# The second FFN product as one level of Strassen, in both layers of a decoder trunk

## Chip, cores and metric

The kernel runs on one core of a Trainium2 chip. The metric is the device time of one execution in microseconds, given as the median of several runs. All data are float32.

## The reference, cut to what matters

Two layers work on 512 tokens of width 1024. Each has a token mixer (gMLP in layer 0, forgetting attention in layer 1) and then a SwiGLU feed-forward block of hidden width 2816, each between two RMS norms with adaLN shift, scale and gate. After layer 0 the keys, values and forget gates of the attention are projected from the residual stream.

```python
def swiglu(h, w_gu, w_down):
    gu = h @ w_gu
    g, u = jnp.split(gu, 2, axis=-1)
    return (jax.nn.silu(g) * u) @ w_down

h = modulate(rms_norm(x, pre_ffn_g[layer]), sh_f, sc_f)
y = swiglu(h, ffn_w_gu[layer], ffn_w_down[layer])
x = x + g_f[:, None, :] * rms_norm(y, post_ffn_g[layer])
```

The change is to the last product of `swiglu`: 512 x 2816 times 2816 x 1024.

## The kernel before, in words

**Split products.** Every float32 operand of a large product is split into two parts of the type fp32r: `hi` is the rounded copy and `lo` the rest (value minus `hi`). A product takes three matmuls: `hi` by `hi`, `hi` by `lo`, `lo` by `hi`. The copy is mostly on ScalarE (in the profile ACT), the subtraction mostly on VectorE (DVE), in some places on GpSimd (POOL). `load_split` (lines 112 to 123) loads one piece of weights of 128 x 1024 into the tile `raw` by a DMA that SyncE (SP) issues, copies it (L118) and subtracts (L122). `raw` has three buffers in the whole kernel, `whi` and `wlo` two in each pool that has them.

**The FFN** (`ffn`, lines 361 to 413). First product: for each of 22 blocks `m` of 128 hidden columns, a gate and an up product of 24 matmuls of 512 columns each (`prods`, L375), with the normalised input as the moving operand, 16 tiles `hT` of the pool `hp`. `act` (lines 377 to 382) then applies Silu (ACT, L379), multiplies (DVE, L380), and stores the hidden block already split: `hi` by ACT (L381), `lo` by POOL (L382). Between these blocks `run_bg` (L174) issues conditioning work from a queue: `ada_block` (lines 181 to 184) loads 128 x 1024 into `rawb`, which has one buffer, and reduces it on DVE (L184). Inside the FFN's pool the tile is `rawb`; elsewhere it is `raw`. Layer 0 has 64 such blocks in the queue, layer 1 has 8.

**Second product** (lines 406 to 413, `moving`, lines 284 to 322). It is taken in two chunks of 512 output columns. In each, 11 pieces of weights (two k-tiles of 128 rows each) are loaded and split; for every k-tile and each of four token tiles come three matmuls (L300, L301, L302), with the hidden block as stationary operand and the weights moving. That is 2 x 22 x 4 x 3 = 528 matmuls of 512 columns in a layer. Of the second chunk the last six pieces are held on chip (four of them by `load_split_h`, lines 128 to 139, in slots of `hp`) and taken token tile by token tile, so that a tile's sums are complete early.

**After it.** For each token tile `residual` (lines 335 to 352) takes the norm and updates x; in layer 0 `boundary` (lines 415 to 425) then makes the next normalised input of two token tiles at a time (`prenorm_half`, lines 268 to 282: scaling, transposes L277, parts by L252 to L259), under high priority. It also keeps the transposed x in SBUF (L282), for a second normalised input in the attention (lines 798 to 802). The next products (lines 707 to 719) take token tiles 0 and 1 first, then 2 and 3. In layer 1 `residual` stores the output.

**What sets the order.** The program is written in Tile: a scheduler puts each engine's instructions in an order by priority (program order, raised by `high_priority`) and by when it reckons that operands and buffers are ready; on the chip each engine then works through its own list in that order and waits by semaphores. SP's list of DMAs is such a list too.

## Time and profile before

| What | us |
|---|---|
| median of 3 runs | 1394.59 |
| lowest, highest run | 1394.45, 1399.97 |
| profiled execution: span, first to last instruction | 1398.4 |
| busy in it: PE | 1353.1 |
| busy: DVE | 811.5 |
| busy: ACT | 542.1 |
| busy: POOL | 269.1 |

The span is of one profiled execution, and the page gives no other time of it; it lies 3.8 us over the median and inside the range of the runs. PE is TensorE's matmul, PEld its load of the stationary operand. The busy time of an engine is a sum over its instructions; what it waited for is seen in the timeline and in the groups.

### The profile page before, as it was taken

To read this page: it belongs to the slowest core of one execution; us is meant where nothing else is said; L and a number is where in the kernel's file an instruction comes from. 1 tells how busy PE (TensorE), PEld (TensorE's weight loads), DVE (VectorE), ACT (ScalarE), POOL (GpSimd) and SP (SyncE) were. 2 spreads that over 40 slices of the span, in tenths; PEclk is the share of its full clock that TensorE was granted. 3 is DMA by queue.
4 is the path that set the end of the run, shared out by engine and by line. 5 is a ranking of instruction groups with operands and counts; after the bars stand their busy time and mean duration, and the time that the engine had idled before them with its cause. 6 is when DMAs were issued, how large, how long until landed. Compare 5 with 4: busy or idle time off the path is not lost.

```text
span 1398.4 us, 17394 instructions
## 1 busy us (share of the span) xinstructions
PE 1353.1 (97%) x6529; PEld 1126.5 (81%) x6529; DVE 811.5 (58%) x1422; ACT 542.1 (39%) x932; POOL 269.1 (19%) x208
## 2 busy tenths in 40 slices
PE   6999999998999999999999899999989999999998
PEld 4788888778888888778798777888788888888886
DVE  7878857756545556553644857888675232231233
ACT  5234433344223232123653346787543232221231
POOL 4700000013111111000110725563031111110000
PEclk9999999999999999999999999999999999999999
DMA  8565436833666666664123231111326333322231
GB/s 322 169 214 156 135 112 200 276 106 113 211 201 198 196 195 212 222 232 136 53 85 105 76 95 42 31 31 46 109 76 207 116 95 93 103 91 75 91 114 67
DMA packets 55237, 189.08 MB, mean 135 GB/s; under 512 B 6769, under 2 KB 7025, under 8 KB 55154
## 3 DMA queue, kind: packets, MB, share of 16 engines
q1 hardware_dynamic: 54578, 186.93, 42.5%
q8 instruction: 51, 0.84, 0.3%
q10 hardware_dynamic: 576, 1.05, 0.2%
q14 instruction: 32, 0.26, 0.1%
HBM read 185.84 MB, written 2.11 MB: 134 GB/s over the span
## 4 chain that ended last, share of the span: by engine, by line
PE 62%; DVE 6%; DMA 5%; issue 2%; ACT 2%; POOL 0%; DVEq 0%; ACTq 0%; POOLq 0%
PE acc L375 32%; PE acc L301 6%; PE acc L302 5%; PE acc L300 5%; DMA rawb<-in_ada_t 4%; PE acc L860 3%; PE acc L948 1%; PE ps_z L901 1%; DVE wlo L122 1%; PE acc L1080 1%; PE acc L1081 1%; PE acc L1079 1%; PE acc L928 1%; DVE rawb L184 1%; PE ps_x L277 1%
## 5 line engine op out<-in xcount | busy, mean ns | idle before, releaser
L375 PE MATMUL acc<-hT,whi 128*128 128x512 f32 (+1 forms) x1536 | 429.6, 373 | 0.0
L118 ACT ACTIVATE whi<-raw 128x1024 fp32r<-128x1024 f32 (+2 forms) x196 | 204.2, 1043 | 538.5 <-PE acc L375 287.0
L122 DVE TENSOR_TENSOR wlo<-raw,whi 128x1024 fp32r<-128x1024 f32 (+2 forms) x196 | 241.0, 1231 | 242.1 <-ACT whi L118 238.6
L375 PEld LDWEIGHTS acc<-hT,whi 128*128 128x128 f32 x1536 | 273.9, 190 | 49.9
L375 PE MATMUL acc<-hT,wlo 128*128 128x512 f32 (+1 forms) x768 | 268.2, 373 | 0.0
L375 PEld LDWEIGHTS acc<-hT,wlo 128*128 128x128 f32 x768 | 137.8, 191 | 24.9
L382 POOL TENSOR_TENSOR hid<-sg,hid 128x512 fp32r<-128x512 f32 (+1 forms) x48 | 73.9, 1540 | 391.7 <-ACT hid L381 391.7
L301 PE MATMUL acc<-wlo,hT 128*128 128x512 f32 (+1 forms) x352 | 136.0, 386 | 5.0 <-DVE wlo L122 5.0
L302 PE MATMUL acc<-whi,hT 128*128 128x512 f32 (+1 forms) x352 | 135.5, 385 | 0.0
L300 PE MATMUL acc<-whi,hT 128*128 128x512 f32 (+1 forms) x352 | 135.0, 385 | 0.0
L184 DVE CUSTOM_DVE_ANT_0 rawb<-rawb,c_bc 128x1024 f32<-128x1024 f32 x62 | 78.3, 1262 | 95.9 <-DMA rawb<-in_ada_t 63.8
L301 PE MATMUL acc<-wlo,hid 128*128 128x512 f32 x288 | 112.6, 391 | 1.2 <-DVE wlo L122 1.2
L300 PE MATMUL acc<-whi,hid 128*128 128x512 f32 x288 | 112.0, 390 | 1.3 <-ACT junk L327 1.3
L302 PE MATMUL acc<-whi,hid 128*128 128x512 f32 x288 | 112.2, 390 | 0.0
L259 POOL TENSOR_TENSOR hT<-hfull,hT 128x256 fp32r<-128x256 f32 (+1 forms) x43 | 44.0, 1034 | 249.5 <-DVE hT L258 124.8
L301 PEld LDWEIGHTS acc<-wlo,hT 128*128 128x128 f32 x352 | 66.4, 189 | 19.4 <-DVE wlo L122 6.9
L300 PEld LDWEIGHTS acc<-whi,hT 128*128 128x128 f32 x352 | 66.5, 189 | 12.7
L302 PEld LDWEIGHTS acc<-whi,hT 128*128 128x128 f32 x352 | 66.5, 189 | 12.5
L380 DVE TENSOR_TENSOR sg<-sg,acc 128x512 f32<-128x512 f32 (+1 forms) x48 | 30.7, 640 | 78.5 <-PE acc L375 78.5
L122 POOL TENSOR_TENSOR wlo<-raw,whi 128x1024 fp32r<-128x1024 f32 x20 | 55.0, 2752 | 79.0 <-DVE whi L120 47.1
L301 PEld LDWEIGHTS acc<-wlo,hid 128*128 128x128 f32 x288 | 54.1, 188 | 13.9 <-DVE wlo L122 2.8
L300 PEld LDWEIGHTS acc<-whi,hid 128*128 128x128 f32 x288 | 53.9, 188 | 13.2 <-ACT junk L327 1.7
(277 smaller groups left out, 2121.0 us busy)
## 6 DMA issues: line engine op xcount, KB each, us to landing
raw<-in_w_gu SPq DMA_DIRECT2D x88, 512.0 KB, 3.6
raw<-in_ada_t SPq DMA_DIRECT2D x50, 512.0 KB, 4.5
rawb<-in_ada_t SPq DMA_DIRECT2D x46, 512.0 KB, 3.9
raw<-in_w_down SPq DMA_DIRECT2D x44, 512.0 KB, 3.6
raw<-in_w_in SPq DMA_DIRECT2D x32, 512.0 KB, 4.0
raw<-in_w_out SPq DMA_DIRECT2D x16, 512.0 KB, 4.3
rawb<-in_kv_ada_t SPq DMA_DIRECT2D x16, 512.0 KB, 3.7
x<-in_x SPq DMA_DIRECT2D x8, 512.0 KB, 6.1
```

The source lines that it names most:

```text
L118: ACT(hi[:, :width], raw[:, :width], AF.Copy)
L122: lo_eng.tensor_tensor(lo[:, :width], raw[:, :width], f32(hi[:, :width]), sub)
L184: nc.vector.tensor_tensor_reduce(raw, raw, c_bc, 1.0, 0.0, mul, add, dst)
L259: last = lo_eng.tensor_tensor(lo, full, f32(hi), sub)
L277: nc.tensor.transpose(ps[:, i, j * P:(j + 1) * P], xr[j][:, kt * P:(kt + 1) * P], ident)
L300: MM(banks[n], lh, wh, start=kt == 0, stop=False)
L301: MM(banks[n], lh, wl, start=False, stop=False)
L302: MM(banks[n], ll, wh, start=False, stop=kt == kts - 1)
L375: MM(o, (hi, hi, lo)[z][:, ks], h[z == 1][kt][:, cs], start=i == 0, stop=i == 3 * KT - 1)
L380: TT(sg, sg, u, mul)
L382: nc.gpsimd.tensor_tensor(hid[1][m][:, cs], sg, f32(hid[0][m][:, cs]), sub)
L860: pin(MM(box[0], (hi, hi, lo)[z][:, cs], h[z == 1][kt], start=kt + z == 0, stop=kt == KT - 1 and z == 2))
```

## The change

Per layer, the second product is written as one level of Strassen (the form with common sums, after Winograd). The tokens are cut into two halves of 256, the hidden columns into even and odd blocks, the output columns into two halves of 512. Seven products of quarters stand for eight, at the price of sums of quarters of the input (`sums`) and of the weights (`t1` to `t4`), and of sums of the products at the end.

The hidden blocks are no longer stored split. `act` writes float32 quarters (two multiplications of 256 columns), `sums` makes four sums of 128 x 256 on POOL for each pair of blocks, and `down` splits quarters and sums (`parts_q`) as it needs them. `down` has a first loop of 11 pieces with four products each (24 matmuls) in all eight PSUM banks, sums of products, a second loop of 11 pieces with three products each (18 matmuls), of which the last four are held and taken tile by tile, in the order 2, 3, 0, 1. The kept transposed x goes to DRAM and back. The next products take token tiles 2 and 3 first. In layer 0 the queue of conditioning work is emptied faster: 67 of its 68 entries in the first product instead of 57. `down` runs inside the pool that has `rawb`. The diff, cut to this (it also takes away comments and docstrings, and passes `y0` tile by tile elsewhere):

```diff
-                nc.scalar.copy(keep[kp][:, :, cs], ps)
+                kst = small.tile([P, 2, 256], F32, name="kst", tag="t2", bufs=3)
+                nc.scalar.copy(kst, ps)
+                nc.sync.dma_start(keep[kp][:, :, cs], kst)
...
-    def residual(n, y0, ps, ss, row, sx):
+    def residual(n, y0, ps, ss, row, sx, raw=1):
...
-            TT(y1, ps, row[:, 512:1024], mul)
+            TT(y1, ps, row[:, raw * 512:raw * 512 + 512], mul)
...
-        for j, y in enumerate((y0[:, n, :], y1)):
+        for j, y in enumerate((y0, y1) if raw else (y1, y0)):
...
+    def down(src, qa, qb, fp, fw, row, done):
+        H = 256
+        NP = NF // 2
+        TAIL = 4
+        ss = fw.tile([P, 2 * NT], F32, name="ss", bufs=1)
+        X, Z = ([acc.tile([P, 512], F32, name="acc") for _ in range(2)] for _ in range(2))
+        Y, W = ([aux.tile([P, 512], F32, name="ps_x", tag=t) for _ in range(2)] for t in ("ps_t", "ps_s"))
+        def parts(w, lo_eng=nc.vector, held=False):
+            if not held:
+                hi, lo = (hp.tile([P, S], F32R, name="hT") for _ in range(2))
+            else:
+                q = held_tile("wq", F32R)
+                hi, lo = q[:, 0], q[:, 1]
+            ACT(hi, w, AF.Copy)
+            lo_eng.tensor_tensor(lo, w, f32(hi), sub)
+            return hi, lo
+        def parts_q(q, n, held):
+            if held:
+                hi, lo = (fp.tile([P, 1024], F32R, name="qh", tag="qb", bufs=NP)[:, :n * H] for _ in range(2))
+            else:
+                hi, lo = (wp.tile([P, 1024], F32R, name=t, tag=t, bufs=2)[:, :n * H] for t in ("whi", "wlo"))
+            ACT(hi, q, AF.Copy)
+            TT(lo, q, f32(hi), sub)
+            return lambda i, t: tuple(x[:, i * H + t * P:i * H + t * P + P] for x in (hi, lo))
+        def prod(bank, a, w, start, stop):
+            (ah, al), (wh, wl) = a, w
+            MM(bank, ah, wh, start=start, stop=False, skip_group_check=True)
+            MM(bank, ah, wl, start=False, stop=False, skip_group_check=True)
+            MM(bank, al, wh, start=False, stop=stop, skip_group_check=True)
+        def half_piece(i):
+            r0 = raw_tile()
+            nc.sync.dma_start(r0[:, :512], src[0, i, :, 512:])
+            return r0[:, :512]
+        def held_tile(name, dt=F32):
+            return fp.tile([P, 2, 512], dt, name=name, tag="qa", bufs=NP)
+        for i in range(NP):
+            r0, r1 = raw_tile(), raw_tile()
+            nc.sync.dma_start(r0, src[0, i])
+            nc.sync.dma_start(r1, src[1, i])
+            t1, t2 = (t[:, z] for t in (fw.tile([P, 2, 512], F32, name="ta", tag="whi"),) for z in range(2))
+            t4 = fw.tile([P, 2, 512], F32, name="tb", tag="wlo")[:, 0]
+            TT(t1, r1[:, :512], r0[:, :512], sub)
+            nc.gpsimd.tensor_tensor(t2, r1[:, 512:], t1, sub)
+            nc.gpsimd.tensor_tensor(t4, r0[:, 512:], t2, sub)
+            a = parts_q(qa[i].rearrange("p q c -> p (q c)"), 4, False)
+            for z, (w, bank, eng) in enumerate(((r0[:, :512], X, nc.vector), (t1, Z, nc.vector), (t2, Y, nc.vector),
+                                                (t4, W, nc.gpsimd))):
+                w = parts(w, eng)
+                for t in range(2):
+                    prod(bank[t], a((3, 1, 2, 0)[z], t), w, i == 0, i == NP - 1)
+            run_bg(1)
+        u2 = held_tile("u2")
+        uw = [held_tile("uw") for _ in range(2)]
+        for t in range(2):
+            nc.scalar.copy(u2[:, t], X[t])
+        for t in range(2):
+            TT(u2[:, t], Y[t], u2[:, t], add)
+        for t in range(2):
+            TT(uw[t][:, 1], Z[t], u2[:, t], add)
+            TT(uw[t][:, 0], W[t], u2[:, t], add)
+        V = [aux.tile([P, 512], F32, name="ps_x", tag="ps_t") for _ in range(2)]
+        held = []
+        for i in range(NP):
+            last = i >= NP - TAIL
+            r1 = raw_tile()
+            nc.sync.dma_start(r1, src[1, i])
+            t3 = fw.tile([P, 2, 512], F32, name="ta", tag="whi")[:, 0]
+            nc.gpsimd.tensor_tensor(t3, r1[:, 512:], r1[:, :512], sub)
+            a = parts_q(qb[i].rearrange("p q c -> p (q c)")[:, H:], 3, last)
+            b22 = parts(r1[:, 512:], held=last)
+            if last:
+                held.append([i, a, b22, parts(t3)])
+                continue
+            b21, w3 = parts(half_piece(i), nc.gpsimd), parts(t3)
+            for t in range(2):
+                prod(Z[t], a(1, t), b22, False, False)
+            for t in range(2):
+                prod(X[t], a(2, t), b21, False, False)
+            for t in range(2):
+                prod(V[t], a(0, t), w3, i == 0, False)
+            run_bg(1)
+        for h in held:
+            h.append(parts(half_piece(h[0]), nc.gpsimd, held=True))
+        g = row()
+        for t in range(2):
+            for i, a, b22, w3, b21 in held:
+                prod(V[t], a(0, t), w3, False, i == NP - 1)
+            n = 2 + t
+            TT(uw[t], V[t].unsqueeze(1).broadcast_to([P, 2, 512]), uw[t], add)
+            sumsq(uw[t][:, 1], ss[:, 2 * n:2 * n + 1])
+            TT(uw[t][:, 1], uw[t][:, 1], g[:, 512:], mul)
+            done(n, uw[t][:, 0], uw[t][:, 1], ss, g, 0)
+        for t in range(2):
+            for i, a, b22, w3, b21 in held:
+                prod(Z[t], a(1, t), b22, False, i == NP - 1)
+            TT(u2[:, t], Z[t], u2[:, t], add)
+            sumsq(u2[:, t], ss[:, 2 * t:2 * t + 1])
+            TT(u2[:, t], u2[:, t], g[:, 512:], mul)
+            for i, a, b22, w3, b21 in held:
+                prod(X[t], a(2, t), b21, False, i == NP - 1)
+            done(t, X[t], u2[:, t], ss, g, 0)
+    def ffn(layer, h, row, done, halves=(0, 1)):
-            hid = [[fp.tile([P, S], F32R, name=f"hid{q}_{m}") for m in range(NF)] for q in range(2)]
+            qa, qb = ([fp.tile([P, 4, H], F32, name=f"q{z}{i}", tag=f"q{z}", bufs=NF // 2) for i in range(NF // 2)]
+                      for z in "ab")
...
-                    TT(sg, sg, u, mul)
-                    ACT(hid[0][m][:, cs], sg, AF.Copy)
-                    nc.gpsimd.tensor_tensor(hid[1][m][:, cs], sg, f32(hid[0][m][:, cs]), sub)
+                    i = m // 2
+                    outs = ((qb[i][:, 3], qa[i][:, 0]) if m % 2 else (qa[i][:, 3], qb[i][:, 0]))
+                    for z, half in enumerate(range(cs.start // H, cs.stop // H)):
+                        TT(outs[half], sg[:, z * H:z * H + H], u[:, z * H:z * H + H], mul)
+                def sums(i):
+                    a22, s1, s2, a11 = (qa[i][:, z] for z in range(4))
+                    a21, s3, s4, a12 = (qb[i][:, z] for z in range(4))
+                    for o, x0, x1, op in ((s1, a21, a22, add), (s2, s1, a11, sub), (s3, a11, a21, sub), (s4, a12, s2, sub)):
+                        nc.gpsimd.tensor_tensor(o, x0, x1, op)
...
+                sums(0)
...
                             with behind_norm():
-                                run_bg(1 if layer else 1 + j)
+                                run_bg(1 if layer else 1 + j + (m % 2) * (1 - j))
                         ps.append(b)
                     act(m, ps[0], ps[1], slice(0, S))
+                    if m % 2:
+                        sums(m // 2)
+                down(w_down[layer], qa, qb, fp, fw, row, done)
                 bgp.pop()
-            with tc.tile_pool(name=f"fd{layer}", bufs=1) as fd:
-                y0 = fd.tile([P, NT, 512], F32, name="y0")
-                ss = fd.tile([P, 2 * NT], F32, name="ss")
-                lhs = hl(hid)
-                moving([w_down[layer, 0, i] for i in range(NF // 2)], NF, 512, lhs, first_half(y0, ss, row))
-                moving([w_down[layer, 1, i] for i in range(NF // 2)], NF, 512, lhs,
-                       lambda n, ps: done(n, ps, y0, ss, row()), tail=6,
-                       tail_load=lambda i, src: load_split_h(src) if i > 1 else cols_of(load_split(src), 512))
...
-        def done(n, ps, y0, ss, row):
+        def done(n, ps, y0, ss, row, raw=1):
...
-                residual(n, y0, ps, ss, row, sx)
+                residual(n, y0, ps, ss, row, sx, raw)
                 xrs(n, sx, rst)
-                if n == 1:
-                    box.append(new_h())
                 if n % 2:
-                    prenorm_half(n // 2, rst, box[0], a, b, keep() if keep else None)
+                    if not box:
+                        box.append(new_h())
+                    prenorm_half(n // 2, rst, box[0], a, b, keep)
...
+    keep = [dram.tile([P, 2, S], F32, name=f"keep{i}", bufs=1) for i in range(4)]
...
-            for grp in ((0, 1), (2, 3)):
+            for grp in ((2, 3), (0, 1)):
...
+                kept = raw_tile().rearrange("p (a s) -> p a s", a=2)
+                nc.sync.dma_start(kept, keep[kt // 2])
                 full2 = small.tile([P, 2, S], F32, name="full2", tag="t4", bufs=2)
-            evac_h(h, kt, slice(0, S), keep[kt // 2][:, kt % 2, :], A1, B1, nc.scalar, nc.vector, nc.gpsimd,
+            evac_h(h, kt, slice(0, S), kept[:, kt % 2, :], A1, B1, nc.scalar, nc.vector, nc.gpsimd,
                    full2[:, kt % 2, :])
```

## Rows read from the trace of the kernel before

**Rows 1.** The core's span (us) and its granted TensorE clock.
```profile
core 0: 1398.4 us, clock 0.988
```

**Rows 2.** The page, part 4: the chain that ended last, by engine.
```profile
PE 62%; DVE 6%; DMA 5%; issue 2%; ACT 2%; POOL 0%; DVEq 0%; ACTq 0%; POOLq 0%
```

**Rows 3.** Windows, second product, each layer: us; PE, PEld, DVE, ACT, POOL busy; clock, DMA, GB/s.
```profile
565.70:691.80 126.10, 123.31 (x545) 100.08 (x544) 64.23 (x115) 39.11 (x66) 3.93 (x4) 1.00 0.50 161
1271.70:1391.60 119.90, 119.90 (x529) 98.78 (x527) 36.03 (x53) 28.48 (x43) 1.29 (x1) 1.00 0.27 88
```

**Rows 4.** Groups of instructions by shape, 1271.7 to 1391.6 us: busy us, mean ns | idle.
```profile
L301 PE MATMUL acc<-wlo,hid 128*128 128x512 f32 x144 | 56.1, 390 | 0.0
L122 DVE TENSOR_TENSOR wlo<-raw,whi 128x1024 fp32r<-128x1024 f32 x16 | 19.6, 1225 | 64.0 <-ACT whi L118 64.0
L118 ACT ACTIVATE whi<-raw 128x1024 fp32r<-128x1024 f32 x16 | 17.0, 1061 | 63.7 <-PE acc L302 63.7
L137 DVE TENSOR_TENSOR hT<-raw,hT 128x512 fp32r<-128x512 f32 x8 | 5.1, 684 | 1.6 <-ACT hT L135 1.6
L135 ACT ACTIVATE hT<-raw 128x512 fp32r<-128x512 f32 x8 | 4.6, 620 | 2.4 <-DMA raw<-in_w_down 2.4
L382 POOL TENSOR_TENSOR hid<-sg,hid 128x512 fp32r<-128x512 f32 x1 | 1.3, 1287 | 9.1 <-ACT hid L381 9.1
```

**Rows 5.** Lines L785 (VectorE) and L788 (GpSimd), side by side: ns min/median/max, first and last start.
```profile
L785 DVE TENSOR_TENSOR k<-k,r x8: 683/1782/1796, 770.9 to 800.4; 128x512 f32<-128x512 f32 x8
L785 DVE TENSOR_TENSOR q<-q,r x4: 682/683/693, 821.9 to 823.8; 128x512 f32<-128x512 f32 x4
...
L788 POOL TENSOR_TENSOR k<-k,kq x8: 1620/1742/2262, 772.7 to 803.3; 128x512 f32<-128x512 f32 x8
```

**Rows 6.** Timeline of the start, 43 to 50 us, VectorE and GpSimd: start, length.
```profile
44.35 2.22 DVE L459 SCALAR_TENSOR_TENSOR A_m<-A_m,b,colv 128x1 f32<-128x1 f32 x1
46.50 1.21 DVE L454 CUSTOM_DVE_ANT_0 raw<-raw,c_bc 128x1024 f32<-128x1024 f32 x1
47.76 1.13 DVE L460 TENSOR_TENSOR B_m<-B_m,colv 128x1 f32<-128x1 f32 x1
...
43.25 3.31 POOL L122 TENSOR_TENSOR wlo<-raw,whi 128x1024 fp32r<-128x1024 f32 x1 [1.51 <-DVE whi L120]
46.52 2.35 POOL L259 TENSOR_TENSOR hT<-hfull,hT 128x512 fp32r<-128x512 f32 x1
49.57 3.30 POOL L122 TENSOR_TENSOR wlo<-raw,whi 128x1024 fp32r<-128x1024 f32 x1 [0.70 <-DVE whi L120]
```

**Rows 7.** Tile rawb, layer 0: ns min/median/max, first and last start; time to landing.
```profile
L184 DVE CUSTOM_DVE_ANT_0 rawb<-rawb,c_bc x54: 1212/1226/1920, 337.4 to 624.9; 128x1024 f32<-128x1024 f32 x54
DMA to landing us min/median/max: 3.3/3.9/5.0
```

**Rows 8.** The page, part 6: loads of the second product, KB each, us to landing.
```profile
raw<-in_w_down SPq DMA_DIRECT2D x44, 512.0 KB, 3.6
```

**Rows 9.** Timeline after token tile 1's last product in layer 0, by engine.
```profile
674.32 0.57 ACT L327 ACTIVATE junk<-acc 128x512 bf16<-128x512 f32 x1
...
687.84 1.32 POOL L259 TENSOR_TENSOR hT<-hfull,hT 128x256 fp32r<-128x256 f32 x1 [117.88 <-DVE rq L169]
695.11 0.81 POOL L259 TENSOR_TENSOR hT<-hfull,hT 128x256 fp32r<-128x256 f32 x1 [0.32 <-DVE rq L168]
...
696.38 0.88 DVE L122 TENSOR_TENSOR wlo<-raw,whi 128x704 fp32r<-128x704 f32 x1
```

**Rows 10.** Timeline of the end: the last product and the last update of x.
```profile
1391.42 0.39 PE L302 MATMUL acc<-hT,hid 128*128 128x512 f32 x1
1394.08 1.42 DVE L348 SCALAR_TENSOR_TENSOR x<-y,rpost,x 128x512 f32<-128x512 f32 x2
```

**Rows 11.** Window 30 to 40 us, columns as in rows 3.
```profile
30.00:40.00 10.00, 6.59 (x21) 4.69 (x21) 9.89 (x11) 2.15 (x4) 9.30 (x4) 0.83 0.72 256
```

More of the change, by code (lines that the diff above doesn't have):

```diff
@@ L126, in cols_of @@
         return lambda j: tuple(t[:, j * nw:(j + 1) * nw] for t in hl_)
-    def load_split_h(src):
-        raw = raw_tile()
-        nc.sync.dma_start(raw, src)
-        parts = []
-        for j in range(2):
-            hi = hp.tile([P, S], F32R, name="hT")
-            ACT(hi, raw[:, j * 512:(j + 1) * 512], AF.Copy)
-            lo = hp.tile([P, S], F32R, name="hT")
-            TT(lo, raw[:, j * 512:(j + 1) * 512], f32(hi), sub)
-            parts.append((hi, lo))
-        return lambda j: parts[j]
     def rsqrt(dst, s0, s1, width):
@@ L358, in hl @@
         return lambda kt, n: (h[0][kt][:, n * P:(n + 1) * P], h[1][kt][:, n * P:(n + 1) * P])
-    def ffn(layer, h, row, done):
+    def down(src, qa, qb, fp, fw, row, done):
[99 more added lines that the diff above has]
+            done(t, X[t], u2[:, t], ss, g, 0)
@@ L363, in ffn @@
+    def ffn(layer, h, row, done, halves=(0, 1)):
+        H = 256
         with tc.tile_pool(name=f"ffn{layer}", bufs=1) as fp:
-            hid = [[fp.tile([P, S], F32R, name=f"hid{q}_{m}") for m in range(NF)] for q in range(2)]
+            qa, qb = ([fp.tile([P, 4, H], F32, name=f"q{z}{i}", tag=f"q{z}", bufs=NF // 2) for i in range(NF // 2)]
+                      for z in "ab")
             with tc.tile_pool(name=f"fw{layer}", bufs=2) as fw:
@@ L379, in act @@
                     ACT(sg, g, AF.Silu)
-                    TT(sg, sg, u, mul)
-                    ACT(hid[0][m][:, cs], sg, AF.Copy)
-                    nc.gpsimd.tensor_tensor(hid[1][m][:, cs], sg, f32(hid[0][m][:, cs]), sub)
+                    i = m // 2
[7 more added lines that the diff above has]
+                        nc.gpsimd.tensor_tensor(o, x0, x1, op)
                 ws = [[load_split(w_gu[layer, m, j], pool=(wp, fw)[m], hi_eng=(None, nc.vector)[m],
                                   lo_eng=(nc.vector, nc.gpsimd)[m]) for j in range(2)] for m in range(2)]
-                for half in range(2):
+                for half in halves:
                     cs = slice(half * 256, half * 256 + 256)
@@ L655, in tile_yoco_trunk @@
         moving([w_out[1, i] for i in range(8)], NG, 512, lambda kt, n: (vh[:, kt, n, :], vl[:, kt, n, :]),
-               lambda n, ps: d0(n, ps, y0, ss, g_m0[0]), tail=5,
+               lambda n, ps: d0(n, ps, y0[:, n, :], ss, g_m0[0]), tail=5,
                tail_load=lambda i, src: cols_of(load_split(src, pool=gp, bufs=5), 512),
@@ L668, in tile_yoco_trunk @@
     kbox = []
-    kp = {}
-    def keep():
-        if not kp:
-            kp["ctx"] = tc.tile_pool(name="attk", bufs=1, side="right")
-            ap = kp["ctx"].__enter__()
-            kp["t"] = [ap.tile([P, 2, S], F32, name=f"keep{i}") for i in range(4)]
-        return kp["t"]
+    keep = [dram.tile([P, 2, S], F32, name=f"keep{i}", bufs=1) for i in range(4)]
     ffn(0, hbox[0], lambda: (run_bg(100), g_f0[0])[1], boundary(sx2, rst2, kbox, Ak, Bk, keep))
-    keep = kp["t"]
     with tc.tile_pool(name="att", bufs=1) as tp:
@@ L799, in tile_yoco_trunk @@
             if kt % 2 == 0:
+                kept = raw_tile().rearrange("p (a s) -> p a s", a=2)
+                nc.sync.dma_start(kept, keep[kt // 2])
                 full2 = small.tile([P, 2, S], F32, name="full2", tag="t4", bufs=2)
-            evac_h(h, kt, slice(0, S), keep[kt // 2][:, kt % 2, :], A1, B1, nc.scalar, nc.vector, nc.gpsimd,
+            evac_h(h, kt, slice(0, S), kept[:, kt % 2, :], A1, B1, nc.scalar, nc.vector, nc.gpsimd,
                    full2[:, kt % 2, :])
-        kp["ctx"].__exit__(None, None, None)
         outer = tp
@@ L1084, in tile_yoco_trunk, with store @@
                         else:
-                            d2(n, bank, y0, ss, g_m1[0])
+                            d2(n, bank, y0[:, n, :], ss, g_m1[0])
     g_f1 = gate_row("f1", ("a", 1, 5), C_POSTF + 8)
-    def store(n, ps, y0, ss, row):
-        residual(n, y0, ps, ss, row, None)
+    def store(n, ps, y0, ss, row, raw):
+        residual(n, y0, ps, ss, row, None, raw)
     ffn(1, fbox[0], lambda: (run_bg(100), g_f1[0])[1], store)
```

## Prediction

> **What bounds the kernel now.** I read the span first: 1398.4 us at a granted clock of 0.988, so full speed (2.4 GHz) nearly throughout [rows 1]. The profiled run lies 3.8 us over the median of 1394.59; I work out a difference against the span and put it on the median. The chain that ended last is PE for 62% [rows 2], so the next view is the two windows of the second FFN product. In layer 1 PE is busy for all of 119.90 us; in layer 0 for 123.31 of 126.10, with DVE busy for half of the time [rows 3]. Of the 529 matmuls in layer 1's window 528 are the product: 119.90 / 529 = 0.2267 us each. The groups of that window show its split work with room to spare: a DVE subtraction of 1024 columns takes 1.225 us, of 512 columns 0.684; the ACT copies take 1.061 and 0.620; a POOL subtraction of 512 columns, alone, 1.287 [rows 4]. PE sets this stage today, and the reader has to ask whether it still will once there is less for PE and more for the others.
>
> **What goes.** Per layer 7 x 11 x 2 x 3 = 462 matmuls stand for 528. The 66 saved are 66 x 0.2267 = 15.0 us, in both layers 29.9: the whole gain.
>
> **What comes, first loop** (11 pieces of 24 matmuls, 24 x 0.2267 = 5.44 us of PE each). Per piece DVE has one subtraction of 1024 columns (the quarters) and four of 512 (t1 and three lo parts): 1.225 + 4 x 0.684 = 3.96 us. POOL has three of 512 (t2, t4, one lo): 3 x 1.287 = 3.86. ACT has 1.061 + 4 x 0.620 = 3.54. Each engine by itself is below 5.44. But each of these DVE and POOL instructions reads two operands in SBUF, and the trace shows that such instructions don't run side by side. Lines L785 (DVE) and L788 (POOL) work next to each other: the DVE one then takes 1.78 us, against 0.683 when POOL is quiet, and the POOL one 1.742, against 1.287 alone [rows 4, 5]. In the start of the kernel a DVE instruction on one element per partition takes 2.22 us: it begins at 44.35 in the middle of a POOL subtraction and ends with it, at 46.57 against 46.56; then L454, begun first, holds up POOL's next one, which takes 2.35 [rows 6]. So their times add. A pair of 512 columns takes 1.742 where the two alone make 0.684 + 1.287 = 1.971: a share of 0.884, since the ends overlap a little. I take this share for all, as rows 5 show the same two kinds of instruction: (3.96 + 3.86) x 0.884 = 6.9 us for a piece, over PE's 5.44. The bounds are 5.44 (no adding up) and 7.82 (the full sum).
>
> The Trainium skill (SBUF — State Buffer, Who interferes with whom) says that a VectorE instruction with two SBUF inputs and a GpSimd instruction that reads SBUF exclude each other for the whole instruction. By that a piece would take the full 7.82 us where the row gives 6.9; what that makes of the time is a rival below, and the pair in rows 5 speaks for 6.9.
>
> The head start is one piece: its `hT` slots and temporaries come free in the last 5.4 us of the first product, so 1.5 of its 6.9 us are left when PE arrives. The last weight sum of piece 10 is ready at 1.5 + 10 x 6.9 = 70.5 us, PE then has 6 matmuls left and ends the loop at 71.9, against 59.8 for PE alone.
>
> **Sums of products.** Two ACT copies and six DVE additions, of which PE has to wait for some 2 us (two to three additions of 0.684 before it may go on in Z). This hides: the second loop's first piece isn't ready before 70.5 + 4.3 = 74.8. If PE set the pace it would cost the 2 us.
>
> **Second loop** (18 matmuls, 4.08 us of PE a piece). DVE: 768 columns, which no row has; between 0.88 for 704 and 1.225 for 1024 [rows 4, 9] I take 0.95, nearest to the first; and two of 512. POOL: two of 512. Together 0.95 + 1.37 + 2.57 = 4.89, times 0.884 = 4.33, again over PE. Piece 6 is ready at 70.5 + 7 x 4.33 = 100.8. The four held pieces need 0.95 + 1.37 + 1.29 = 3.61, times 0.884 = 3.19 each before V can be finished: 113.6. The first thing that PE's list has after piece 6 is V of the held pieces, so it waits for them. Then 3 matmuls and 60 more: 63 x 0.2267 = 14.3, end at 127.9. Before it was 119.9: **8 us longer** in each layer.
>
> **The end of a tile.** A tile of the lower half now needs an addition of 1024 columns and a gain more on DVE, about 1.9 us, and four tiles come 2.7 us apart or 5.4, not 8.2. The queue on DVE makes the last update of x about 1 us later than today's 1394.08 - 1391.42 = 2.7 us after the last product [rows 10]. Layer 1: 8 + 1 = +9.
>
> **Conditioning blocks in layer 0.** They go through one buffer: 54 begin from 337.4 to 624.9, one in 5.42 us, with 3.9 us of that for the load [rows 7]. Issuing them earlier in the program doesn't speed up a ring of one buffer, and ten or so that used `raw` now use it too. 64 at 5.42 us end at 678.9; the second product begins at 565.7 [rows 3], so 21 of them fall into it. Before, DVE had 62 us of idle time there. Now each holds the shared path for 1.226 x 0.884 = 1.08 us: +23 us. Bounds: 0 (all hidden in waits) and 21 x 2 = 42 (DVE also stands before each one until its load lands, with the splits queued behind it).
>
> **The boundary after layer 0.** From tile 1's last product to the last part of the next input of that half 21.6 us pass (674.32 to 695.92) [rows 9]. Covering it were the 72 matmuls of tiles 2 and 3 (16.3 us); now it is the 48 of tiles 0 and 1 (10.9). The next product can begin on its first k-tiles, so I take 4 of the missing 5.4 us. Bounds 0 and 10, as DVE now has more queued there.
>
> **Priced at nothing.** The hidden block's second multiplication and POOL's four sums of 256 columns (0.81 each [rows 9]) take the place of a copy and a split, under 48 matmuls (10.9 us) a block. The kept x: the ACT copy stays, eight stores of 256 KB and four loads of 512 KB (3.6 us to land [rows 8]) stand in SP's list by weight loads that are due 16 us later; without that cover a load's 3.6 us. Loads of weights: 1 MB in 6.9 us is 152 GB/s, below the 161 that layer 0 has today [rows 3]. PSUM: the next product waits until X is read; within the boundary's bounds.
>
> **Sum:** 9 + 8 + 23 + 4 = +44 us: 1394.6 + 44 = **1439 us**.
>
> **Rivals.**
> - *PE stays the limit* (faster). DVE and POOL overlap enough that a piece of the first loop needs under 5.44 us, 70% of the full sum; that is the point from which it decides. For it: each engine alone has 30% idle, and PE alone is the chain today. Against it: rows 5 and 6. Then -29.9, two waits of 2 for sums of products, two ends of 1 and 4 at the boundary: -20, 1375 us. Chance 0.18.
> - *In between.* Handing over is cheaper and a piece takes 6.0 us, and the blocks of layer 0 hide: 9 + 8 + 4 - 2 x 9 = +3, 1398 us. Chance 0.07.
> - *The blocks hide, the rest stands.* +21, 1416 us. Rows 7's 3.9 us of load leave DVE free to split meanwhile. Chance 0.12.
> - *The ring of three `raw` buffers.* Each piece takes two, and the next r1 goes into the buffer that t4 of this one frees: t1, t2, t4 and a load are 0.68 + 1.29 + 1.29 + 3.6 = 6.9 us [rows 4, 8] with nothing in between; with two other DVE instructions let in first, 0.6 each, 8.1. Then 10 x 1.2 us more a layer: +68, 1463 us. Chance 0.12.
> - *Full exclusion*, 7.82 and 4.89 us a piece, and 3.61 a held one: the first loop's last sum at 2.4 + 78.2 = 80.6, the held pieces at 80.6 + 34.2 + 14.4 = 129.2, end at 143.5, that is +23.6 a layer for +8, and 3 for the blocks: +78, 1473 us. Chance 0.08. This is the rule named above (Trainium skill, SBUF — State Buffer) taken to the letter.
>
> PE's pauses could also bring its clock down: in one window with PE busy for 6.59 of 10 us the grant is 0.83, so part of it at 1.2 GHz [rows 11]. In the first loop PE would be busy for 5.44 of 6.9 us. I put up to 10 us for it into the upper end only.
>
> **How the numbers follow.** The forecast, 1416 to 1456 by its own bounds, has 0.43. The range goes from 1392 (in between, less a few us) to 1476 (ring and most of full exclusion) and leaves out the fast rival and a little above. This kernel can tell 0.5%, 7 us, from no change: faster 0.18, same 0.07, slower 0.12 + 0.43 + 0.12 + 0.08 = 0.75.
>
> **What would show it.** In the changed profile: PE busy near 80% in the first loop with waits for DVE or POOL subtractions; POOL's 512-column subtractions at about 1.7 us and many DVE ones over 1 us; one idle stretch of PE some 10 us long, all told, ahead of the held pieces; `rawb` still loading in layer 0's second product. I am wrong if PE is dense in both loops (then POOL at 1.29 and DVE at 0.68), or if its waits end on a load of `raw` (the ring).

## The result, and the profile after

The changed kernel takes 1458.9 us (median of 4 runs, 1458.41 to 1459.71) against 1395.66 for the kernel before beside it: a ratio of 1.0439, 95% interval 1.0415 to 1.0462. It is slower by 63 us where the prediction said 44; 1458.9 lies in its wide range of 1392 to 1476, and just above the 1416 to 1456 that the forecast gave itself by its own bounds. The profiled run is the 1458.41 one, its span 1456.7 us, 58.3 over the span of [rows 1].

The chain that ended last in the kernel after, by engine (before: [rows 2]):

```profile
PE 35%; DVE 11%; issue 5%; POOL 4%; ACT 3%; DMA 3%; DVEq 0%; POOLq 0%; ACTq 0%; SPq 0%
```

PE's share falls from 62% to 35%. To find where the 58.3 us lie, cut the span at the same events in both kernels: first and last matmul of each second product, and the last of the first v products. Windows of the kernel after, columns as in [rows 3]: layer 0's second product, from its end to the end of the first v products, layer 1's second product, its first loop alone, what follows that loop, and the end.

```profile
563.30:718.80 155.50, 122.06 (x463) 92.27 (x462) 144.59 (x152) 64.95 (x102) 90.08 (x56) 0.91 0.61 197
718.80:772.90 54.10, 40.26 (x226) 38.36 (x227) 33.63 (x96) 31.70 (x70) 11.45 (x12) 0.84 0.35 113
1315.00:1446.80 131.80, 112.84 (x463) 85.60 (x461) 115.44 (x114) 66.36 (x110) 91.17 (x56) 0.99 0.46 142
1315.00:1390.70 75.70, 64.84 (x266) 49.39 (x264) 67.74 (x56) 36.71 (x57) 59.82 (x37) 0.98 0.48 146
1390.70:1446.80 56.10, 47.99 (x199) 36.21 (x197) 47.70 (x59) 29.65 (x54) 31.36 (x20) 1.00 0.43 136
1446.80:1456.70 9.90, 0.00 (x0) 0.00 (x0) 6.75 (x17) 1.61 (x5) 0.00 (x0) 0.66 0.43 159
```

The kernel before has the second of these as:

```profile
691.80:728.20 36.40, 34.53 (x211) 34.15 (x211) 20.42 (x57) 21.75 (x43) 7.62 (x10) 0.95 0.32 99
```

| stretch | before | after | difference | predicted |
|---|---|---|---|---|
| up to layer 0's second product | 565.7 | 563.3 | -2.4 | 0 |
| layer 0, second product | 126.1 | 155.5 | +29.4 | +31 |
| boundary and first v products | 36.4 | 54.1 | **+17.7** | +4 |
| attention, layer 1's first product | 543.5 | 542.1 | -1.4 | 0 |
| layer 1, second product | 119.9 | 131.8 | +11.9 | +8 |
| end | 6.8 | 9.9 | +3.1 | +1 |
| span | 1398.4 | 1456.7 | +58.3 | +44 |

(58.3 and not 63, mostly as the profiled run of before was 3.8 us over the median.) In layer 1's product the count of matmuls fell by 66, yet the product takes 11.9 us more: PE is busy for only 112.84 of 131.80 us, DVE for 115.44 (36.03 of 119.90 before [rows 3]). What each does in the first loop, groups by shape (the last column is idle time and what ended it):

```profile
L371 DVE TENSOR_TENSOR hT<-ta,hT 128x512 fp32r<-128x512 f32 x21 | 30.6, 1457 | 5.9 <-ACT hT L370 5.4
L371 POOL TENSOR_TENSOR hT<-tb,hT 128x512 fp32r<-128x512 f32 x11 | 20.9, 1904 | 7.5 <-ACT hT L370 7.5
L388 PE MATMUL acc<-hT,wlo 128*128 128x512 f32 x44 | 18.7, 425 | 9.0 <-DVE wlo L381 9.0
L405 POOL TENSOR_TENSOR ta<-raw,ta 128x512 f32<-128x512 f32 x10 | 16.0, 1603 | 6.8 <-DVE ta L404 6.8
L406 POOL TENSOR_TENSOR tb<-raw,ta 128x512 f32<-128x512 f32 x10 | 16.0, 1599 | 0.7
L404 DVE TENSOR_TENSOR ta<-raw 128x512 f32<-128x512 f32 x10 | 13.2, 1324 | 1.2 <-DMA raw<-in_w_down 0.8
L371 DVE TENSOR_TENSOR hT<-raw,hT 128x512 fp32r<-128x512 f32 x12 | 12.2, 1017 | 0.9 <-PE ps_x L387 0.7
```

A subtraction of 512 columns that takes DVE 0.684 us alone [rows 4] takes 1.02 to 1.46 in the mean here, POOL's 1.60 to 1.90 for 1.287. Only 0.8 us of DVE's idle time ahead of t1 ends on a load; PE's longest wait ends on DVE's part of the quarters (L381). The timeline shows them taking turns:

```profile
1338.33 1.68 POOL L405 TENSOR_TENSOR ta<-raw,ta 128x512 f32<-128x512 f32 x1 [0.62 <-DVE ta L404]
1339.03 1.52 DVE L371 TENSOR_TENSOR hT<-ta,hT 128x512 fp32r<-128x512 f32 x1 [0.18 <-ACT hT L370]
1340.09 1.63 POOL L406 TENSOR_TENSOR tb<-raw,ta 128x512 f32<-128x512 f32 x1
1340.71 1.55 DVE L371 TENSOR_TENSOR hT<-ta,hT 128x512 fp32r<-128x512 f32 x1 [0.15 <-ACT hT L370]
```

POOL's first ends at 1340.01, DVE's at 1340.55; POOL's second at 1341.72, DVE's at 1342.26. Each DVE instruction ends 0.54 us after the POOL one beside which it began, as if it did its work once POOL is through. From the first matmul of piece 1 (1321.1) to that of piece 10 (1382.8) are nine pieces of 6.85 us, predicted 6.9. In the second loop POOL stands 11.6 us, all told, ahead of the sum t3 for loads of `raw`; no run sets apart what that costs.

In layer 0's second product the blocks go on loading, 21 of them as predicted, the last at 716.5 us (tile rawb):

```profile
L171 DVE CUSTOM_DVE_ANT_0 rawb<-rawb,c_bc x21: 1198/1214/2348, 567.0 to 716.5; 128x1024 f32<-128x1024 f32 x21
```

That blocks run into this product is not new: in the kernel before 18 began in it, the last at 624.9 [rows 7], and PE was still busy for 123.31 of 126.10 us [rows 3]. What is new is that DVE is full there.

And the boundary, the stretch that was mis-sized. DVE after the V products of tiles 2 and 3, with the first part of the next input, and PE's first v product:

```profile
708.11 1.23 DVE L451 TENSOR_TENSOR uw<-ps_x,uw 128x1024 f32<-128x1024 f32 x1 [0.82 <-PE ps_x L388]
709.25 1.21 DVE L171 CUSTOM_DVE_ANT_0 rawb<-rawb,c_bc 128x1024 f32<-128x1024 f32 x1
711.00 1.77 DVE L453 TENSOR_TENSOR uw<-uw,grow 128x512 f32<-128x512 f32 x1
712.69 1.24 DVE L151 SCALAR_TENSOR_TENSOR rq<-ss 128x1 f32<-128x1 f32 x1
716.45 1.20 DVE L171 CUSTOM_DVE_ANT_0 rawb<-rawb,c_bc 128x1024 f32<-128x1024 f32 x1
719.38 0.75 DVE L338 SCALAR_TENSOR_TENSOR x<-y,rpost,x 128x512 f32<-128x512 f32 x1
724.45 0.75 DVE L338 SCALAR_TENSOR_TENSOR x<-y,rpost,x 128x512 f32<-128x512 f32 x1
733.07 0.27 DVE L245 CAST hT<-hfull 128x256 fp32r<-128x256 f32 x1
733.40 0.66 PE L817 MATMUL acc<-whi,hT 128*128 128x352 f32 x1
```

The sum of tile 2 begins at 708.11, its x at 719.38, tile 3's at 724.45. PE ends the product at 718.8 and begins the next at 733.40; in between it has only transposes. Two blocks, and two instructions held up while POOL has the path (1.77 us, and 1.24 for one element per partition), stand in DVE's queue. In the first v products, 733.4 to 772.9, PE waits for the split v weights (us in total, times, longest):

```profile
PE acc L817 <- ACT whi L118: 1.7, 1, 1.7
PE acc L818 <- DVE wlo L122: 1.3, 2, 0.7
```

### The profile page after: what moved, and what is told of

Its sections match the earlier page's. It is cut to its first block, busy times and chain, and to the rows that moved or that the text cites. A ratio compares the mean times of both kernels' runs of the same rounds, so it can differ in the third digit from the quotient of the medians.

```text
span 1456.7 us, 17922 instructions
## 1 busy us (share of the span) xinstructions
PE 1349.4 (93%) x6397; PEld 1108.9 (76%) x6397; DVE 999.8 (69%) x1606; ACT 599.5 (41%) x1034; POOL 488.4 (34%) x358
## 4 chain that ended last, share of the span: by engine, by line
PE 35%; DVE 11%; issue 5%; POOL 4%; ACT 3%; DMA 3%; DVEq 0%; POOLq 0%; ACTq 0%; SPq 0%
PE acc L482 15%; PE acc L963 3%; DVE hT L371 2%; DMA raw<-in_w_down 2%; PE acc L290 1%; PE acc L291 1%; PE acc L289 1%; PE acc L1051 1%; PE ps_z L1004 1%; POOL tb L406 1%; POOL ta L405 1%; DVE wlo L122 1%; DVE wlo L381 1%; PE acc L1183 1%; ACT hT L370 1%
## 5 line engine op out<-in xcount | busy, mean ns | idle before, releaser
L118 ACT ACTIVATE whi<-raw 128x1024 fp32r<-128x1024 f32 (+2 forms) x160 | 166.0, 1039 | 438.0 <-PE acc L482 303.5
L122 DVE TENSOR_TENSOR wlo<-raw,whi 128x1024 fp32r<-128x1024 f32 (+2 forms) x160 | 196.6, 1230 | 145.1 <-ACT whi L118 143.1
L171 DVE CUSTOM_DVE_ANT_0 rawb<-rawb,c_bc 128x1024 f32<-128x1024 f32 x72 | 101.1, 1404 | 73.5 <-DMA rawb<-in_ada_t 49.7
L371 DVE TENSOR_TENSOR hT<-ta,hT 128x512 fp32r<-128x512 f32 x66 | 89.8, 1364 | 9.1 <-ACT hT L370 8.2
L496 POOL TENSOR_TENSOR qa<-qb,qa 128x256 f32<-128x256 f32 x22 | 35.7, 1625 | 172.5 <-DVE qa L490 172.5
L496 POOL TENSOR_TENSOR qb<-qa,qb 128x256 f32<-128x256 f32 x22 | 35.7, 1622 | 159.1 <-DVE qb L490 159.1
L388 PE MATMUL acc<-hT,wlo 128*128 128x512 f32 x144 | 61.8, 431 | 27.5 <-DVE wlo L381 27.5
L290 PEld LDWEIGHTS acc<-wlo,hT 128*128 128x128 f32 x352 | 66.4, 189 | 17.8 <-DVE wlo L122 5.2
L370 ACT ACTIVATE hT<-ta 128x512 fp32r<-128x512 f32 x66 | 41.5, 629 | 87.7 <-DVE ta L404 52.5
L386 PE MATMUL acc<-hT,whi 128*128 128x512 f32 x144 | 60.2, 418 | 12.0 <-DVE uw L421 6.7
L387 PE MATMUL acc<-hT,whi 128*128 128x512 f32 x144 | 59.8, 415 | 3.8 <-POOL hT L371 2.6
```

The costliest lines, as they stand in the source:

```text
L118: ACT(hi[:, :width], raw[:, :width], AF.Copy)
L122: lo_eng.tensor_tensor(lo[:, :width], raw[:, :width], f32(hi[:, :width]), sub)
L171: nc.vector.tensor_tensor_reduce(raw, raw, c_bc, 1.0, 0.0, mul, add, dst)
L290: MM(banks[n], lh, wl, start=False, stop=False)
L371: lo_eng.tensor_tensor(lo, w, f32(hi), sub)
L386: MM(bank, ah, wh, start=start, stop=False, skip_group_check=True)
```

## The experiments

**1. All subtractions of the second product on DVE.**

```
-nc.gpsimd.tensor_tensor(t2, r1[:, 512:], t1, sub)
-nc.gpsimd.tensor_tensor(t4, r0[:, 512:], t2, sub)
+TT(t2, r1[:, 512:], t1, sub)
+TT(t4, r0[:, 512:], t2, sub)
```

(and so for t3 and the lo parts of t4 and b21)

> All the subtractions of the second product that POOL had (t2, t4, t3 and the lo parts of t4 and b21) go to DVE; POOL has none left there. Theory (DVE and POOL take turns on a shared path, so that their times add): a piece of the first loop then costs DVE 3.96 + 3 x 0.684 = 6.0 us with nothing beside it, against 6.9 now, although DVE has more to do; its 512-column subtractions fall from 1.0 to 1.5 us to 0.68. In layer 1 the first loop goes from 75.7 us to 66 to 69, the second product from 131.8 to 117 to 121; in layer 0 the second product from 155.5 to 139 to 144; the kernel from 1459 to 1426 to 1435. Rival 1 (the engines work independently, and DVE's long times are its own): DVE gets three more of 1.36 us a piece, 6.6 + 4.1 = 10.7, the first loop of layer 1 takes over 110 us and the kernel over 1520. Rival 2 (the buffers of the loads set the pace): DVE goes on waiting and the kernel stays within 10 us of 1459.

Measured: 1417.1 us, ratio to before 1.0145 (1.0122 to 1.0168), 42 us below the changed kernel. Windows of layer 1's second product and of its first loop, then a whole piece on DVE:

```profile
1294.30:1405.20 110.90, 107.36 (x463) 87.39 (x461) 106.25 (x167) 65.81 (x110) 3.25 (x3) 0.98 0.52 171
1294.30:1354.20 59.90, 59.90 (x266) 49.51 (x265) 58.53 (x86) 35.31 (x56) 3.25 (x3) 1.00 0.55 180
```

```profile
1320.13 1.22 DVE L381 TENSOR_TENSOR wlo<-qa,whi 128x1024 fp32r<-128x1024 f32 x1
1321.27 0.69 DVE L371 TENSOR_TENSOR hT<-ta,hT 128x512 fp32r<-128x512 f32 x1
1321.87 0.68 DVE L371 TENSOR_TENSOR hT<-tb,hT 128x512 fp32r<-128x512 f32 x1
...
1325.62 1.22 DVE L381 TENSOR_TENSOR wlo<-qa,whi 128x1024 fp32r<-128x1024 f32 x1
```

With more to do, DVE is faster: eight instructions in 5.49 us, and PE is dense in the first loop (59.9 of 59.9 us, 5.45 a piece). Layer 1's product takes 110.9 us, less than the 117 to 121 expected, and the kernel less than its 1426 to 1435; layer 0's product, 138.2, comes out just under its 139 to 144. The reason: a DVE instruction of 0.68 us begins 0.60 us after the one ahead of it, that of 1.22 is followed after 1.14. So the 6.0 us that was added up from durations is really 1.14 + 7 x 0.60 = 5.3, below PE's 5.44. Rivals 1 and 2 fall.

**2. Subtractions on POOL that nobody needs,** on top of experiment 1.

```
+for _ in range(3):
+    nc.gpsimd.tensor_tensor(tb[:, 1], r1[:, 512:], r0[:, 512:], sub)
```

> All subtractions of the second product on DVE, and POOL gets three subtractions of 512 columns for each piece of the first loop whose result nobody reads, as many as it had there. Theory (taking turns on a shared path): they still cost, though nothing waits for them: a piece of the first loop goes from 5.45 us to 8.2 to 9.0, DVE's 512-column subtractions from 0.685 to 1 us or more in the mean; the kernel from 1417 to 1475 to 1500. Rival (what cost 6.9 us was the chain t1, t2, t4 that went from DVE to POOL and back, its latency and its waits): the piece stays at 5.4 to 5.6 us and the kernel at 1417 to 1423.

Measured: 1482.8 us (one run); a piece of layer 1's first loop takes 8.9 us (1334.8 to 1414.8 for nine). Groups in that loop:

```profile
L409 POOL TENSOR_TENSOR tb<-raw 128x512 f32<-128x512 f32 x30 | 49.7, 1657 | 35.5 <-DMA raw<-in_w_down 30.4 <-DVE hT L371 3.6
L371 DVE TENSOR_TENSOR hT<-ta,hT 128x512 fp32r<-128x512 f32 x23 | 25.8, 1129 | 0.0
L406 DVE TENSOR_TENSOR ta<-raw,ta 128x512 f32<-128x512 f32 x10 | 16.9, 1694 | 0.0
```

No result of L409 is read, and each of the three costs a piece (8.9 - 5.45) / 3 = 1.15 us. So it is the shared path, not the chain over two engines. Nor is it the loads that POOL's reads of `raw` might hold back: DVE is busy for 78.5 of these 80.0 us.

**3. The sums left out.**

```
-nc.gpsimd.tensor_tensor(t2, r1[:, 512:], t1, sub)
-nc.gpsimd.tensor_tensor(t4, r0[:, 512:], t2, sub)
+t2, t4 = r1[:, 512:], r0[:, 512:]
...
-nc.gpsimd.tensor_tensor(t3, r1[:, 512:], r1[:, :512], sub)
+t3 = r1[:, :512]
```

> Leaves out the sums t2, t4 and t3 (raw quarters are multiplied in their place), and the lo parts that POOL had go to DVE: the same number of matmuls and of loads, but DVE has 3.96 + 0.684 = 4.6 us a piece in the first loop and 3.0 in the second, POOL nothing. Theory (the shared path of DVE and POOL sets the pace, not PE, the loads or the buffers): PE sets the pace, 5.44 and 4.08 us a piece; layer 1's second product takes 105 to 109 us for 131.8 now, layer 0's 116 to 123 for 155.5, the kernel 1390 to 1402. Rival (the loads' buffers or PE's clock set the pace): pieces of the first loop stay above 6.3 us and the kernel above 1430.

Measured: 1430.9 us (one run), layer 1's product 122.0 us, a piece 6.11: a miss, and in the kernel's time (above 1430) what the rival said, though the piece stays below its 6.3. With less work than in experiment 1 it is slower. Groups of layer 1's first loop:

```profile
L380 ACT ACTIVATE whi<-qa 128x1024 fp32r<-128x1024 f32 x9 | 9.5, 1052 | 10.2 <-PE ps_x L387 10.2
L404 DVE TENSOR_TENSOR ta<-raw 128x512 f32<-128x512 f32 x10 | 6.9, 692 | 15.0 <-DMA raw<-in_w_down 15.0
```

DVE stands 15.0 us ahead of t1 until a load lands (0.8 in the changed kernel). The edit changed more than it meant to: t2 and t4, as tiles of their own, had set `raw` free early; now the raw quarters stay until their parts are made, and these wait for slots that PE frees. That is read from the trace alone; a run with a fourth raw buffer, which would test it, was not made. Since the edit opened a new wait, the run decides neither for the theory nor against it.

**4. The last 22 conditioning blocks left out.**

```
+nblk[0] += 1
+if 42 < nblk[0] <= 64:
+    nc.vector.memset(dst, 0.0)
+    return
```

> Leaves out the last 22 conditioning blocks of layer 0 (their loads and their reductions; zeros stand in their columns), which are those that fall into its second product. Theory (each holds the shared path, which sets the pace there): layer 0's second product falls from 155.5 us to layer 1's 130 to 134, and the stretch from its end to the end of the first v products from 54.1 to 46 to 50, as three of the blocks stand in front of the updates of x there; the kernel takes 1427 to 1433. Rival (DVE does them in waits that it has anyway): the product stays at 150 or more, the kernel at 1452 or more.

Measured: 1434.4 us (one run), 24.0 below the profiled run of the changed kernel. Windows of the product and of the boundary:

```profile
564.40:704.10 139.70, 116.77 (x467) 87.89 (x465) 117.19 (x121) 71.58 (x121) 89.81 (x56) 0.96 0.45 143
704.10:748.60 44.50, 38.23 (x221) 36.26 (x222) 26.75 (x77) 24.76 (x52) 11.54 (x12) 0.92 0.40 129
```

The size of the term was right (+23), though the kernel came out just above its 1427 to 1433. By these windows 15.8 us come out of the product (130 to 134 was expected, it is 139.7) and 9.6 out of the boundary (44.5, for 46 to 50). But the cut misleads here: ahead of the last five matmuls of the product PE stands 4.5 us for the scaled x of the next input, a wait of the boundary that now lies in the product. From the product's first matmul to the sum of tile 2 it took 144.8 us and now takes 119.5; from that sum to the first v product it took 25.3 and takes 25.7 (4.5 of them DVE stands for a part of the v weights). So all of the gain lies ahead of that sum.

**5. The edits of experiments 1 and 4 together.**

```
-nc.gpsimd.tensor_tensor(t2, r1[:, 512:], t1, sub)
+TT(t2, r1[:, 512:], t1, sub)
...
+if 42 < nblk[0] <= 64:
+    nc.vector.memset(dst, 0.0)
+    return
```

> Both edits: all subtractions of the second product on DVE, and the last 22 conditioning blocks of layer 0 left out (zeros in their columns). Theory: both layers' second products take 117 to 121 us; the stretch from the end of layer 0's to the end of the first v products falls from 54.1 to 42 to 47, because neither blocks nor POOL stand in DVE's way, and what is left over the 36.2 us of before is the shorter cover (48 matmuls for 72, 5.4 us); the kernel takes 1395 to 1404. Rival for that stretch (the order of the tiles and the cover alone make the delay, not DVE's backlog): it stays at 51 us or more, here and without the blocks alone.

Measured: 1386.6 us (one run), below the kernel before. The products take 108.1 and 111.1 us, below what was expected for the reason found in experiment 1. But the boundary keeps 50.3: there the theory missed, and the rival (51 or more) came close in this run, though not in experiment 4 (44.5), to which it also laid claim. DVE's backlog is the smaller part of the boundary's loss: 3.8 of 17.7 us go with it.

**6. The blocks early.** All subtractions on DVE, nothing left out.

```
-raw = bgp[-1].tile([P, 1024], F32, name="rawb", bufs=1) if bgp else raw_tile()
+if bgp and len(bg) % 3:
+    raw = small.tile([P, D], F32, name="rawt", tag="t4", bufs=2)
+else:
+    raw = bgp[-1].tile([P, 1024], F32, name="rawb", bufs=1) if bgp else raw_tile()
-run_bg(1 if layer else 1 + j + (m % 2) * (1 - j))
+run_bg(1 if layer else 2)
```

> All subtractions of the second product on DVE, and the conditioning blocks of layer 0 issued two to a weight load of the first product, through three buffers (the one of before and the two of xr, which are free there), so that all 64 should be through before the second product. Nothing is left out. Theory (the blocks cost where DVE is full, and nothing where it has room): layer 0's second product takes 108 to 113 us as without the blocks (138 with them), the first product no more than 3 us longer, the kernel 1386 to 1393. Rival (the blocks cost their DVE time and their loads' time wherever they stand): the first product grows by 15 us or more and the kernel stays above 1402.

Measured: 1386.0 us, ratio to before **0.9922** (0.9901 to 0.9943). Windows of the first product, the second, the boundary, and layer 1's second:

```profile
324.00:563.30 239.30, 237.02 (x1108) 199.33 (x1109) 159.64 (x251) 63.26 (x77) 58.73 (x48) 0.99 0.69 235
563.30:671.20 107.90, 105.74 (x463) 86.27 (x461) 104.56 (x162) 67.23 (x112) 3.26 (x3) 1.00 0.56 181
671.20:720.40 49.20, 37.86 (x226) 35.43 (x227) 28.99 (x86) 28.58 (x61) 11.52 (x12) 0.93 0.38 121
1263.10:1374.80 111.70, 107.47 (x463) 87.23 (x462) 106.00 (x167) 65.84 (x110) 3.26 (x3) 0.98 0.52 171
```

The first product takes 239.3 us, as in the kernel after, with all 64 blocks in it: there they are free. Against the span of before: -18.2 in layer 0's product, -8.2 in layer 1's, +12.8 at the boundary, +1.7 at the end, -3.2 elsewhere: -15.1 (between the medians -10.8).

**7. More cover at the boundary.** On experiment 6, the Z and X products of one more piece wait behind V.

```
+if i == NP - TAIL - 1:
+    held.append([i, a, b22, w3, b21])
+    continue
...
-for h in held:
+for h in held[1:]:
```

> The kernel with early blocks, and in both layers the Z and X products of piece 6 put off to the end, behind the V products that finish tiles 2 and 3: the cover of the boundary after layer 0 is 60 matmuls for 48, 2.7 us more. Theory (about 10 us of PE's idle time there is the short cover): PE's idle time ahead of the first v product falls by 2 to 3 us, the kernel by as much against the one with early blocks. Rival (the chain of DVE and ACT is held up by other work, and gets longer by as much): no change within 1 us at the boundary.

Measured: 1385.0 us, 0.9907 (0.9889 to 0.9925), not to be told from experiment 6. PE's idle time between the products is 10.1 us (670.8 to 680.9) for 9.9: a miss, and what the rival said. V's last matmul ends 1.7 us earlier (658.6 for 660.3) and has 53 matmuls behind it for 48, where 60 were meant, but DVE's sum begins only 0.65 us earlier, as its queue has two lo parts of held pieces ahead of it, and the rest of the chain gives that back.

**8. Less cover,** on experiment 6.

```
-TAIL = 4
+TAIL = 2
```

> The kernel with early blocks, with two held pieces for four in both layers, so that 24 matmuls for 48 (5.4 us less) stand behind the V products that finish tiles 2 and 3. Nothing is left out. Theory (PE's idle time at the boundary is the chain from V's last product, 21 us, less what PE has left then): the chain stays at 20 to 22 us, PE's idle time ahead of the first v product goes from 9.9 to 14 to 16 us, the kernel from 1386 to 1389 to 1393. Rival (the chain starts when DVE's queue lets it, not when V is done, as putting off piece 6 suggested): the chain gets shorter by what leaves the queue, the idle time stays within 2 us of 9.9.

**9. A shorter chain.** On experiment 6, a constant for the root and the reciprocal of the sums of squares.

```
+if not raw and sx is not None:
+    nc.vector.memset(r, 1.0)
...
```

> The kernel with early blocks; at the boundary after layer 0 the root and the reciprocal of the sums of squares are left out for all four tiles (a constant 1 in their place), everything else stays. This takes a table load, a root, a reciprocal and three small DVE instructions with their handovers out of each tile's chain, 1.5 to 3 us. Theory (the chain of small DVE and ACT instructions of tiles 2 and 3 in turn is what PE waits for): the chain falls from 21 us to 15 to 18, PE's idle time from 9.9 to 4 to 7 us, the kernel from 1386 to 1379 to 1383. Rival (the first splits of the v weights or their loads are what comes last): idle time and kernel stay within 1.5 us.

The first sum of tile 2 and the first v product in experiments 6, 8 and 9, in this order (in the table the chain is the time between the two, the cover what PE still has of the product in it, the rest is PE's idle time):

```profile
659.56 2.35 DVE L454 TENSOR_TENSOR uw<-ps_x,uw 128x1024 f32<-128x1024 f32 x2
681.09 0.63 PE L820 MATMUL acc<-whi,hT 128*128 128x352 f32 x1
```

```profile
668.46 1.22 DVE L454 TENSOR_TENSOR uw<-ps_x,uw 128x1024 f32<-128x1024 f32 x1
688.00 0.62 PE L820 MATMUL acc<-whi,hT 128*128 128x352 f32 x1
```

```profile
664.31 2.35 DVE L457 TENSOR_TENSOR uw<-ps_x,uw 128x1024 f32<-128x1024 f32 x2
682.90 0.64 PE L823 MATMUL acc<-whi,hT 128*128 128x352 f32 x1
```

| kernel | tile 2's sum begins | product ends | first v product | chain | cover | PE idle |
|---|---|---|---|---|---|---|
| after | 708.1 | 718.8 | 733.4 | 25.3 | 10.7 | 14.6 |
| 6 | 659.6 | 671.2 | 681.1 | 21.5 | 11.6 | 9.9 |
| 8 | 668.5 | 672.8 | 688.0 | 19.5 | 4.3 | 15.2 |
| 9 | 664.3 | 675.9 | 682.9 | 18.6 | 11.6 | 7.0 |

Experiment 8 takes 1391.5 us (one run), and PE's idle time is 15.2, both as expected: less cover, more idle (in layer 1 its product is 4.9 us shorter and its end 5.2 longer, which cancel). The chain, 19.5, came out just under its 20 to 22. Experiment 9 shortens the chain by 2.9 us and the idle time by as much (18.6 and 7.0, at the edge of what was expected; the x of tiles 2 and 3 now come 2.5 us apart for 5.3), but takes 1385.7 us (one run), where 1379 to 1383 was expected: its second product came out 2.6 us longer and began 2.2 us later, for reasons not looked into. So the stretch bears the theory out and the kernel's time doesn't decide. In the kernel before, tile 1's last product is done by 674.32 [rows 9] and the first v product comes 17.8 us later, right behind PE's last matmul of the old product. That is PE's list, not the chain: the first part of the next input lay ready at 687.67, after 13.4 us, and tile 0's x had been updated before tile 1's last product:

```profile
669.69 1.41 DVE L348 SCALAR_TENSOR_TENSOR x<-y,rpost,x 128x512 f32<-128x512 f32 x2
687.38 0.29 DVE L258 CAST hT<-hfull 128x256 fp32r<-128x256 f32 x1
692.08 0.32 PE L715 MATMUL acc<-whi,hT 128*128 128x352 f32 x1
```

**10. Strassen in layer 1 alone,** all its subtractions on DVE; `ffn_old` is the FFN of before.

```
-ffn(0, hbox[0], lambda: (run_bg(100), g_f0[0])[1], boundary(sx2, rst2, kbox, Ak, Bk, keep))
+ffn_old(0, hbox[0], lambda: (run_bg(100), g_f0[0])[1], boundary(sx2, rst2, kbox, Ak, Bk, keep))
-for grp in ((2, 3), (0, 1)):
+for grp in ((0, 1), (2, 3)):
```

> Layer 0's FFN and the boundary behind it as in the kernel before; Strassen in layer 1 alone, with all its subtractions on DVE. Nothing is left out. Theory (the terms of the two layers and of the boundary add): layer 1 gives 119.9 - 110.9 = 9 us and loses 2 at the end; against before -6 to -8, so 1388 to 1391. Rival (layer 1 is paid back in the attention or at the start of its product, as other buffers and loads move): within 3 us of before.

Measured: 1388.8 us, 0.9942 (0.9922 to 0.9962), as expected: the terms add, within a few us (its product took 107.2 us, not 110.9). Layer 0 brings little more, since the boundary takes back 12.8 of its 18.2: experiment 6 is 2.8 us lower, and the two intervals overlap.

## Why the prediction was right, and where it wasn't

- **DVE and POOL share a path: right.** A piece of layer 1's first loop took 6.85 us (6.9), 21 blocks fell into layer 0's second product (21), POOL's subtractions took 1.6 to 1.9 us, and PE was busy for 86% of that loop (near 80% was said). Experiments 1 and 2 settle it: without POOL's work the piece falls to PE's pace, with idle work of POOL's it rises to 8.9.
- **The share of 0.884** was right in size, not in what it was taken for. It stood for ends that overlap at the handover; but of the 0.97 us between 7.82 and 6.85 some 0.4 is that each of the five DVE durations overlaps its own neighbour's by 0.08 us. With starts for durations and experiment 2's price, 4 x 0.60 + 1.14 + 3 x 1.15 = 7.0 us. The rule of the Trainium skill (SBUF — State Buffer, Who interferes with whom), taken with 7.82 us as a rival, is borne out as to the exclusion; what was wrong was to add up durations. The Trainium skill (Perfetto Trace Analysis, DVE / Act Engine Instruction) says that the profiled time of such an instruction lasts until its writes are acknowledged, while the next may begin to fetch before; the rows agree, 0.68 us long and 0.60 apart.
- **Layer 1, +9, measured +15:** 11.9 in the product and 3.1 at the end. The first loop took 75.7 us for 71.9. What the loop lost, it lost at its ends: into its start fall POOL's last three sums of 256 columns, 3.5 us that were priced at nothing, and the third piece takes 8.2 us; the last takes 7.9, with the first sums t3 of the second loop in it. This fits, but no run took them away. What follows the loop took 56.1 us for 56.0, and there the agreement is luck: the one idle stretch of PE, some 10 us long, ahead of the held pieces did not come (PE waits 1.0 us there); the 8.1 us that PE is idle are ten waits of at most 1.3 us, most of them for parts ahead of that. The end of a tile was sized at 1 us and is 3.1.
- **Blocks, +23: right** (24.0 in experiment 4, all of it ahead of tile 2's sum). The 1.08 us for each and the waits behind its load were not taken apart.
- **The boundary, +4 with bounds of 0 and 10: wrong, +17.7.** The step that failed is "the next product can begin on its first k-tiles, so I take 4 of the missing 5.4". It kept the chain of before (21.6 us to the last part; with DVE's own last part, which ends at 696.4, it was 22.1) and set it against fewer matmuls; but the chain itself got longer. To the first part of the next input it took 13.4 us and takes 25.2, and the cover fell from 17.5 to 10.7, so that PE stands 14.6 us. Some 4 us of the chain go with POOL's subtractions and the blocks (21.5 without both; 22.5 in experiment 1, where only the subtractions are gone). The other 8 fit what the timeline shows: tiles 2 and 3 now end one behind the other, and their x come 5.1 us apart, each a string of small DVE and ACT instructions in turn, where before tile 0's was through when tile 1's began. Taking some of these out of each tile shortens the chain (experiment 9); that the tiles' ends lie so close was not varied. The rest of the 17.7 are the first v products themselves, 39.5 us for 36.1. In them PE stands 3.0 us for the split v weights. The granted clock is 0.92 there, for 0.95 before, but experiment 6 has 0.99 and takes 39.3 us all the same: it is not the clock that makes them longer.
- **The ring of `raw`: fell** (0.8 us of waiting in the first loop, to which it was put), though experiment 3 shows that it is close, and the kernel's 1458.9 us is nearer to its 1463 than to the forecast's 1439: by the number alone it would have been believed.
- **PE's clock:** 0.91 in layer 0's second product for 1.00 [rows 3], 0.98 in layer 1's first loop; experiment 6 has layer 0's back at 1.00. The loss came with the waits and wasn't separated from them; of the 63 us a part may be the clock's.
